# A decoder layer on one core: key weights split one product later, a store on another queue, sums in another ring, a shorter block of passes ahead of the first scores

## The chip, the cores and the metric

One Trainium2 chip, one of its cores. The metric is the device time of one execution in microseconds (us), the median of several runs. TensorE is the matrix engine (PE in the rows, its weight loads PEld), VectorE is DVE, ScalarE is ACT, GpSimd is POOL. SyncE (SP) issues nearly all transfers; its rows carry "SPq". A pass below is one matmul with 128 x 128 stationary and 512 moving columns.

## What is computed

One layer of a hybrid decoder, in float32, for one sequence of 1024 tokens and 1024 channels. Cut to what matters here:

```python
h = rms_norm(x, norm_mix_pre)
proj = h @ w_in                     # q_d | k_d | v_d | u_pool | q_mem | gate logits
a = diff_attention(q_d, k_d, v_d, lam)          # 8 heads, two softmax maps each
y_attn = rms_norm(a, subln_g) * (1 - lam_init) @ w_attn_branch
y_pool = multiscale_pool(u_p, ...) @ w_pool_branch
y_mem  = memory_cross_attention(q_m, ...) @ w_mem_branch
gates  = sigmoid(gate_logits)                   # three gates of 1024 channels
mix = gates[0] * y_attn + gates[1] * y_pool + gates[2] * y_mem
x = x + rms_norm(mix @ w_out, norm_mix_post)
x = x + rms_norm(conv_ffn(rms_norm(x, norm_ffn_pre)), norm_ffn_post)
```

The change lies between the gates of the pool and memory branches and the first head of the attention. Nothing of what is computed changes.

## The kernel before

Every float32 operand is split into two parts, hi and lo, that TensorE multiplies: `split` (lines 83 to 92) writes hi with ScalarE (line 86, or 89 with a scale) and lo with VectorE (line 87, or 90), and `mm3` (lines 94 to 97) makes three passes: hi by hi, hi by lo, lo by hi. The projection products of this part use Strassen-like schemes with seven products in place of eight. Pages of split weights go through two rings of two buffers each in the pool `wst` (tags "wh" and "wl", used in turn), raw weights through a ring "raw" of two there and one more buffer in the pool `grp`.

The order of instructions on each engine and of transfers on each queue is not the program's order alone. A planner takes the program's order as priority and lets an instruction go ahead when its own estimates say that inputs and buffers are ready; `tc.issue_after(ins)` holds an instruction behind another on the same engine. What is planned is then executed strictly in that order on each engine and each queue, with semaphores.

The stages around the change, in order of time:

1. **Gates of two branches** (lines 609 to 629, up to about 418 us). For four pairs of channel blocks and two branches, `seven` makes the gate logits into `g` (ring "g" of three buffers of 1 MB in the pool `gp_`), ScalarE takes the sigmoid (line 623), VectorE multiplies by the branch `y` (ring "y" of two buffers of 1 MB, line 624), and the second branch is added to the first (line 628). The sum `mix` is stored to `mixp_d` by SyncE's queue (line 629).
2. **Values** (lines 637 to 738, about 418 to 506 us). Four loads of 1 MB bring the value weights `vw` (line 644) into buffers of the rings "g" and "y". `value_product` (lines 655 to 664) splits four pages and makes 48 passes into four PSUM banks. The products go in the order B11, B21, T2, T1, T3, B22, T4; between them PSUM is copied or added into `vtmp` (ring "g") and back into `vw`. `value_combination` (line 681) makes sums of weight blocks on VectorE. `key_weights(h)` (lines 666 to 676) loads the weights of head h's keys (line 670), splits them into two pages of the same rings "wh" and "wl", and stores these to `wk_d` (line 676). It is called for heads 2 to 7: 2 after B11, 3 after B21, 4 after T2, 5 after T1, 6 after T3, 7 after B22.
3. **Keys and queries** (lines 740 to 772, about 506 to 627 us). `channels` calls `seven` for two channel blocks at a time; `split_heads` splits the result into `hl` (ring "y") and stores it (line 758). The first group and the last, gate channels C_G, keep their four weight sums `ss` in a buffer of the ring "y"; the others in the pool `gq`. `weight_sums` (lines 194 to 197) makes them.
4. **Start of the attention** (lines 1009 to 1070, from about 627 us). The gate of channel block 2 is a generator `gate(2)`, here `first`: 48 passes in four steps of 12, the second and fourth ending with a copy and a store (lines 867 and 868). Two of its steps stand ahead of the first scores (lines 1015 and 1024), and `first_scores` is held behind the last of their passes by `issue_after`. The other steps are fillers of head 0: `weave` deals fillers out among the stages of a head. Scores are line 898, their bias and minimum VectorE's line 901, the exponential line 906, the turned weights line 936, values line 953.

The bias of a head is made by ScalarE from a ramp that GpSimd writes (lines 784 to 791). The keys of head 0 are loaded by line 826, its queries by line 815, its values by line 804.

Of the kernel before, what the change touches and what calls it, by code (L numbers as in the profile page):

```python
# [8 lines left out]
F32 = mybir.dt.float32  # L9
# [6 lines left out]
P = 128  # L16
# [3 lines left out]
H4 = KT // 2  # L20
# [18 lines left out]
def kernel(  # L39
# [7 lines left out]
    nc = tc.nc  # L47
# [12 lines left out]
    out = out[0]  # L60
# [245 lines left out]
    mixp_d = dram.tile([KT, P, S], F32, name="mixp_d")  # L306
# [31 lines left out]
    def chunk(w, c0, n=P):  # L338
        return w[:, c0:c0 + n].rearrange("(k p) c -> p k c", p=P)
# [10 lines left out]
    with tc.tile_pool(name="kvm", reuse_waits="tile", bufs=1, side="right") as kvp:  # L350
# [59 lines left out]
        with tc.tile_pool(name="xa", reuse_waits="tile", bufs=2, side="right") as xa:  # L410
# [81 lines left out]
            for j in range(MH):  # L492
# [9 lines left out]
                fillers = [lambda i=i: pool_in(j, i) for i in range(2)]  # L502
# [106 lines left out]
    with tc.tile_pool(name="gp", reuse_waits="tile", bufs=2, side="right") as gp_:  # L609
        for dt in range(0, KT, 2):  # L610
            mix = None
            for b in (1, 0):
                raws = []
                for e in range(2):
                    w = (grp if e else wst).tile([P, KT, P], F32, tag="raw", name="rawg", bufs=2 - e)
                    nc.sync.dma_start(out=w, in_=chunk(w_in, C_G + (2 - b) * D + (dt + e) * P))
                    raws.append(w)
                y = gp_.tile([P, 2, S], F32, tag="y", name="y")
                nc.sync.dma_start(out=y, in_=branch_d[b][dt:dt + 2].rearrange("e p s -> p e s"))
                g = gp_.tile([P, 2, S], F32, tag="g", name="g", bufs=3)  # L620
                s12, s43 = [gq.tile([P, 2, H4, P], F32, tag="t", name="s") for _ in range(2)]
                seven(raws, (s12[:, 0], s12[:, 1], s43[:, 0], s43[:, 1]), hop, g)
                sigmoid = nc.scalar.activation(out=g, in_=g, func=AF.Sigmoid)
                nc.vector.tensor_tensor(out=g, in0=g, in1=y, op=ALU.mult)
                if b == 1:
                    mix = g
                else:
                    nc.vector.tensor_tensor(out=mix, in0=mix, in1=g, op=ALU.add)
            nc.sync.dma_start(out=mixp_d[dt:dt + 2].rearrange("e p s -> p e s"), in_=mix)

# [18 lines left out]
        def vblock(a, b):  # L651

            return [vw[a][k // 2][:, k % 2, b] for k in range(4)]

        def value_product(name, ws, acc, fresh):
            for k in range(4):
                page = wst.tile([P, 2, H], F32R, tag=("wh", "wl")[pages[0] % 2], name="vpage")
                pages[0] += 1
                split(page[:, 0], page[:, 1], ws[k])
                bh, bl = hop(name, k)  # L660
                for t in TS:
                    ts = slice(t * P, (t + 1) * P)
                    mm3(acc[t], bh[:, ts], bl[:, ts], page[:, 0], page[:, 1], fresh and k == 0, k == 3,
                        onto=not fresh)

        def key_weights(h):

            raw = wst.tile([P, KT, P], F32, tag="raw", name="rawk", bufs=2)
            with tc.issue_after(loads["v"].ins):
                nc.sync.dma_start(out=raw, in_=chunk(w_in, C_K + h * P))  # L670
            for e in range(2):
                page = wst.tile([P, 2, H4, P], F32R, tag=("wh", "wl")[pages[0] % 2], name="kpage")
                pages[0] += 1
                ks = slice(e * H4, (e + 1) * H4)
                split(page[:, 0], page[:, 1], raw[:, ks])
                nc.sync.dma_start(out=wk_d[h, :, :, ks], in_=page.bitcast(F32))
# [22 lines left out]

        A11, A21, A12, A22 = (0, 0), (0, 1), (1, 0), (1, 1)  # L700
        value_product("B11", vblock(*A11), va, True)
        key_weights(2)
        for t in TS:
            nc.scalar.activation(out=vtmp[:, t], in_=va[t], func=AF.Copy)
        value_product("B21", vblock(*A12), vb, True)
        key_weights(3)
        for t in TS:
            nc.vector.tensor_tensor(out=vtmp[:, t], in0=vb[t], in1=vtmp[:, t], op=ALU.add)
        value_combination(A21, A21, A22, ALU.add)
        value_combination(A11, A21, A11, ALU.subtract)  # L710
        value_product("T2", vblock(*A11), va, False)
        key_weights(4)
        for t in TS:
            value_out(t, 0, vtmp[:, t])
        value_product("T1", vblock(*A21), vb, True)
        key_weights(5)
        for t in TS:
            nc.scalar.activation(out=vtmp[:, t], in_=va[t], func=AF.Copy)
# [41 lines left out]
        ss = gp_.tile([P, 4, H4, P], F32, tag="y", name="ss")  # L760
# [1 line left out]
        for h in range(0, NH, 2):  # L762
            split_heads(channels(h * P), q_d[h:h + 2], -0.125)

        ss = gp_.tile([P, 4, H4, P], F32, tag="y", name="ss")
        g01 = [gq.tile([P, S], F32, tag="t", name="g01") for _ in range(2)]
        late = []
        channels(C_G, ss=[ss[:, j] for j in range(4)], g=g01, late=late)
# [237 lines left out]
    def steps(gen, n):  # L1006
        return [lambda: next(gen, None)] * n
# [5 lines left out]
    first = gate(2)  # L1013
# [7 lines left out]
    with tc.issue_after(last["load"].ins):  # L1021
        for dt in range(2):
            nc.sync.dma_start(out=gate_d[dt], in_=g01[dt])
    next(first)
    GATES = ((2,), (), (), (), (), (), (), (3,))
    blocks = [(h, b) for h in range(NH) for b in range(4)]
    for h in range(NH):
        stages = []
        for b in range(4):
            n = 4 * h + b  # L1030
            if n == 0:
                def first_scores():
                    with tc.issue_after(last["gate"].ins):
                        scores(0, 0, 0)
                stages.append(first_scores)
            else:
                stages.append(lambda h=h, b=b: scores(h, b, 0))
            if b == 1 and h + 1 < NH:
                stages.append(lambda h=h: head_bias(h + 1))
            if n >= 1:  # L1040
                def weights(n=n):
                    combine(*blocks[n - 1], 1)
                    turn_weights(*blocks[n - 1])
                stages.append(weights)
            stages.append(lambda h=h, b=b: scores(h, b, 1))
            stages.append(lambda h=h, b=b: combine(h, b, 0))
            if n >= 2:
                stages.append(lambda n=n: head_norm(*blocks[n - 2]))
            if n >= 1:
                stages.append(lambda n=n: weigh_values(*blocks[n - 1]))  # L1050
            if h == HG and b == 0:
                stages.append(lambda: turn_sums(0))
            if h == HG and b == 1:
                stages.append(lambda: load_norms(0))
            if h == HG and b == 3:
                def norms():
                    with tc.issue_after(last["combine"].ins):
                        head_norms(0)
                stages.append(norms)
            if b in (1, 3) and h + 1 < NH:  # L1060
                stages.append(lambda h=h, b=b: queries(h + 1, b // 2))
        fillers = []
        if h + 1 < NH:
            if h:
                fillers += steps(head_keys(h + 1), 4)
            for n, step in enumerate(steps(values(h + 1), 2)):
                fillers.insert(2 * n + 1, step)
        for dt in GATES[h]:
            fillers += steps(first if dt == 2 else gate(dt), 2 if dt == 2 else 4)
        weave(stages, fillers)  # L1070
    combine(*blocks[-1], 1)
    turn_weights(*blocks[-1])
# [47 lines left out]
    for dt in range(KT):  # L1120
        wh, wl, _ = wsplit(chunk(w_attn_branch, dt * P), [P, KT, P])
        for i in range(2):
            hs = slice(i * H, (i + 1) * H)
            gm2 = gq.tile([P, 2, H], F32, tag="t", name="gm2")
            g, mp = gm2[:, 0, :], gm2[:, 1, :]
# [66 lines left out]
    with tc.tile_pool(name="wo", reuse_waits="tile", bufs=1, side="right") as wo:  # L1192
# [3 lines left out]
        for t in range(KT):  # L1196
# [19 lines left out]
            y = yp.tile([P, D], F32, tag="y", name="y", bufs=3)  # L1216
# [284 lines left out]
```

## Time and profile before

| | |
|---|---|
| median of 3 runs | 1764.55 us (1763.64 to 1766.16) |
| profiled execution, time | 1765.92 us |
| its span in the trace | 1763.9 us |
| mean granted TensorE clock | 0.994 |
| TensorE matmul busy | 1718.4 us, 97% |
| VectorE busy | 1274.2 us, 72% |
| ScalarE busy | 884.4 us, 50% |
| GpSimd busy | 45.6 us, 3% |
| DMA share of SyncE's queue | 51.1% |

The busy times are of one profiled execution; the span is what the trace covers, and the execution's time lies 2 us above it. A wait is put down to the instruction or transfer that came last. In the rows a start is in us from the beginning of the span, a length in us, and a line of `split` or `mm3` is that of the helper, so the tile names tell the stage.

### The profile page before, as it was taken

To read this page: it belongs to the slowest core of one execution; us is meant where nothing else is said; L and a number is where in the kernel's file an instruction comes from. 1 tells how busy PE (TensorE), PEld (TensorE's weight loads), DVE (VectorE), ACT (ScalarE), POOL (GpSimd) and SP (SyncE) were. 2 spreads that over 40 slices of the span, in tenths; PEclk is the share of its full clock that TensorE was granted. 3 is DMA by queue.
4 is the path that set the end of the run, shared out by engine and by line. 5 is a ranking of instruction groups with operands and counts; after the bars stand their busy time and mean duration, and the time that the engine had idled before them with its cause. 6 is when DMAs were issued, how large, how long until landed. Compare 5 with 4: busy or idle time off the path is not lost.

```text
span 1763.9 us, 22641 instructions
## 1 busy us (share of the span) xinstructions
PE 1718.4 (97%) x8138; PEld 1424.6 (81%) x8138; DVE 1274.2 (72%) x2227; ACT 884.4 (50%) x1551; POOL 45.6 (3%) x103
## 2 busy tenths in 40 slices
PE   6999999997999999999999999999999999999997
PEld 5888888886888778888888888888888888788886
DVE  7766875665575567888865557858888888878476
ACT  6434454433444366777743333545555555543452
POOL 0000000000000011111110000000000000000000
PEclk9999999999999999999999999999999999999999
DMA  7784544454675576665556472374334323583343
GB/s 243 251 304 145 181 152 132 153 165 132 215 224 188 176 210 179 190 166 159 149 188 222 159 235 72 119 229 135 113 103 126 118 74 108 186 297 103 112 138 138
DMA packets 232933, 294.95 MB, mean 167 GB/s; under 512 B 15873, under 2 KB 161526, under 8 KB 230134
## 3 DMA queue, kind: packets, MB, share of 16 engines
q1 hardware_dynamic: 229302, 286.13, 51.1%
q0 software_dynamic: 3520, 7.38, 1.2%
q8 instruction: 64, 1.05, 0.2%
q14 instruction: 47, 0.39, 0.1%
HBM read 201.62 MB, written 85.56 MB: 163 GB/s over the span
## 4 chain that ended last, share of the span: by engine, by line
PE 75%; issue 13%; DVE 4%; DMA 4%; POOL 2%; ACT 2%; SPq 0%; POOLq 0%; DVEq 0%; ACTq 0%
PE pa L95 8%; PE pa L96 8%; PE pa L97 8%; PE pb L95 5%; PE pb L97 5%; PE pb L96 5%; PE pe L97 2%; PE pe L95 2%; PE pe L96 2%; PE pya L96 2%; PE pya L95 2%; PE pya L97 2%; PE pd L95 2%; PE pd L97 2%; PE pd L96 2%
## 5 line engine op out<-in xcount | busy, mean ns | idle before, releaser
L86 ACT ACTIVATE wpage<-s 128x512 fp32r<-128x512 f32 x136 | 85.2, 627 | 106.8 <-DVE s L194 42.8
L87 DVE TENSOR_TENSOR wpage<-s,wpage 128x512 fp32r<-128x512 f32 x136 | 92.7, 688 | 44.8 <-ACT wpage L86 44.8
L1279 DVE SCALAR_TENSOR_TENSOR cvt<-gv,cols,cvt 128x1023 f32<-128x1023 f32 x88 | 112.5, 1278 | 15.6 <-ACT cvt L1275 15.6
L901 DVE CUSTOM_DVE_ANT_0 z<-pss,hbias 128x256 f32<-128x256 f32 (+7 forms) x128 | 94.9, 752 | 27.9 <-PE pss L898 26.7
L906 ACT ACTIVATE z<-z,mx 128x256 f32<-128x256 f32 (+7 forms) x128 | 98.9, 774 | 21.3 <-DVE mx L901 21.1
L95 PE MATMUL pa<-T,wpage 128*128 128x512 f32 x264 | 102.8, 389 | 1.2 <-DVE gv L252 1.2
L96 PE MATMUL pa<-T,wpage 128*128 128x512 f32 x264 | 102.7, 389 | 0.0
L97 PE MATMUL pa<-T,wpage 128*128 128x512 f32 x264 | 102.7, 389 | 0.0
L898 PE MATMUL pss<-ks,q 128*128 128x512 f32 (+5 forms) x384 | 88.7, 352 | 1.2 <-DVE mx L901 1.2
L86 ACT ACTIVATE page<-blk 128x1024 fp32r<-128x1024 f32 (+1 forms) x42 | 41.4, 988 | 85.7 <-PE pe L96 50.6
L87 DVE TENSOR_TENSOR page<-blk,page 128x1024 fp32r<-128x1024 f32 (+1 forms) x42 | 47.5, 1131 | 38.6 <-ACT page L86 38.6
L898 PEld LDWEIGHTS pss<-ks,q 128*128 128x128 f32 x384 | 62.4, 189 | 12.3 <-DVE mx L901 7.6
L86 ACT ACTIVATE wh<-raw 128x1024 fp32r<-128x1024 f32 (+1 forms) x46 | 41.8, 910 | 60.5 <-PE pb L96 13.7
L95 PE MATMUL pd<-page 128*128 128x512 f32 x176 | 68.6, 390 | 1.7 <-ACT row L1389 1.7
L96 PE MATMUL pd<-page 128*128 128x512 f32 x176 | 68.5, 389 | 0.0
L97 PE MATMUL pd<-page 128*128 128x512 f32 x176 | 68.5, 389 | 0.0
L95 PE MATMUL pa<-hT,wpage 128*128 128x512 f32 x168 | 65.7, 391 | 0.1
L97 PE MATMUL pa<-hT,wpage 128*128 128x512 f32 x168 | 65.4, 389 | 0.0
L96 PE MATMUL pa<-hT,wpage 128*128 128x512 f32 x168 | 65.4, 389 | 0.0
L953 PEld LDWEIGHTS poa<-aT,v 128*128 128x128 f32 x480 | 60.5, 190 | 4.8 <-ACT srow L973 2.5
L953 PE MATMUL poa<-aT,v 128*128 128x256 f32 (+1 forms) x480 | 63.2, 281 | 0.8 <-ACT srow L973 0.5
L87 DVE TENSOR_TENSOR wl<-raw,wh 128x1024 fp32r<-128x1024 f32 (+1 forms) x46 | 47.6, 1034 | 18.5 <-ACT wh L86 18.4
(415 smaller groups left out, 5050.7 us busy)
## 6 DMA issues: line engine op xcount, KB each, us to landing
q<-q_d SPq DMA_DIRECT2D x64, 256.0 KB, 5.3
wd<-in_w_down_dram SPq DMA_DIRECT2D x22, 512.0 KB, 6.2
tw_d<-wd SPq DMA_DIRECT2D x11, 1024.0 KB, 4.5
rawv<-in_w_up_dram SPq DMA_DIRECT2D x22, 512.0 KB, 5.6
rawu<-in_w_up_dram SPq DMA_DIRECT2D x22, 512.0 KB, 3.9
ff_d<-cvt SPq DMA_DIRECT2D x22, 512.0 KB, 4.2
blk<-ff_d SPq DMA_DIRECT2D x20, 512.0 KB, 7.0
br<-tw_d SPq DMA_DIRECT2D x20, 512.0 KB, 3.5
```

The lines of the kernel that those rows point to most:

```text
L86: copy = nc.scalar.activation(out=hi, in_=src, func=AF.Copy)
L87: nc.vector.tensor_tensor(out=lo, in0=src, in1=hi.bitcast(F32), op=ALU.subtract)
L95: nc.tensor.matmul(o, ah, bh, start=first, stop=False, skip_group_check=onto)
L96: nc.tensor.matmul(o, ah, bl, start=False, stop=False, skip_group_check=onto)
L97: return nc.tensor.matmul(o, al, bh, start=False, stop=last, skip_group_check=onto)
L898: nc.tensor.matmul(pss[:, i * H:i * H + m], q[:, j, c, ts], keys, start=(j == 0), stop=(j == 1))
L901: nc.vector.tensor_tensor_reduce(out=halves(z[:, 0:n]), in0=pss.rearrange("p (a m) -> p a m", a=2)[:, 0:parts, 0:m], in1=halves(biases[h][ ...
L906: nc.scalar.activation(out=z[:, 0:n], in_=z[:, 0:n], func=AF.Exp, scale=-1.0, bias=mx[:, c:c + 1], accum_out=sm if c else sums[:, h, t:t + 1])
L953: nc.tensor.matmul(po[:, qs], (vh, vl)[i][:, k, :], w[j][:, ws], start=(n == 0), stop=(n == len(terms) - 1))
L1279: nc.vector.scalar_tensor_tensor(out=cv[:, sh:], in0=u[:, 0:S - sh], scalar=w, in1=cv[:, sh:], op0=ALU.mult, op1=ALU.add)
```

## The change

Four edits. The store of `mix` goes from SyncE's queue to GpSimd's. In the values stage the calls of `key_weights` for heads 2, 3 and 4 each move behind the next product, so that two of them (4 and 5) follow T1. The weight sums of the last group of channels go from the ring "y" to the ring "g". The second step of `first` is no longer made ahead of the first scores: it becomes a filler of head 0, which has three steps of it in place of two.

```diff
@@ gates of two branches
-            nc.sync.dma_start(out=mixp_d[dt:dt + 2].rearrange("e p s -> p e s"), in_=mix)
+            nc.gpsimd.dma_start(out=mixp_d[dt:dt + 2].rearrange("e p s -> p e s"), in_=mix)
@@ values
         value_product("B11", vblock(*A11), va, True)
-        key_weights(2)
         for t in TS:
             nc.scalar.activation(out=vtmp[:, t], in_=va[t], func=AF.Copy)
         value_product("B21", vblock(*A12), vb, True)
-        key_weights(3)
+        key_weights(2)
         for t in TS:
             nc.vector.tensor_tensor(out=vtmp[:, t], in0=vb[t], in1=vtmp[:, t], op=ALU.add)
         value_combination(A21, A21, A22, ALU.add)
         value_combination(A11, A21, A11, ALU.subtract)
         value_product("T2", vblock(*A11), va, False)
-        key_weights(4)
+        key_weights(3)
         for t in TS:
             value_out(t, 0, vtmp[:, t])
         value_product("T1", vblock(*A21), vb, True)
+        key_weights(4)
         key_weights(5)
@@ last group of channels
-        ss = gp_.tile([P, 4, H4, P], F32, tag="y", name="ss")
+        ss = gp_.tile([P, 4, H4, P], F32, tag="g", name="ss", bufs=3)
         g01 = [gq.tile([P, S], F32, tag="t", name="g01") for _ in range(2)]
@@ start of the attention
     with tc.issue_after(last["load"].ins):
         for dt in range(2):
             nc.sync.dma_start(out=gate_d[dt], in_=g01[dt])
-    next(first)
@@ fillers of a head
         for dt in GATES[h]:
-            fillers += steps(first if dt == 2 else gate(dt), 2 if dt == 2 else 4)
+            fillers += steps(first if dt == 2 else gate(dt), 3 if dt == 2 else 4)
```

## Rows read from the trace of the kernel before

**Rows 1.** The page, part 1: busy us, share of the span, instructions of each engine.
```profile
PE 1718.4 (97%) x8138; PEld 1424.6 (81%) x8138; DVE 1274.2 (72%) x2227; ACT 884.4 (50%) x1551; POOL 45.6 (3%) x103
```

**Rows 2.** Waits over the whole span: us in total, times, longest.
```profile
PE ve L95 <- ACT vpage L86: 9.8, 1, 9.8
PE pb L95 <- ACT wpage L86: 3.1, 1, 3.1
...
ACT vpage L86 <- DMA wk_d<-kpage: 12.2, 9, 2.5
```

**Rows 3.** Busy us of each engine in four stretches, then granted clock, DMA share, GB/s.
```profile
428.00:444.00 16.00, 6.20 (x19) 4.46 (x18) 9.28 (x10) 4.88 (x9) 0.00 (x0) 0.68 0.87 272
444.00:500.00 56.00, 56.00 (x249) 46.34 (x248) 37.58 (x57) 30.06 (x52) 0.00 (x0) 1.00 0.73 224
598.00:616.00 18.00, 14.91 (x53) 11.33 (x52) 8.74 (x12) 6.84 (x10) 0.00 (x0) 0.81 0.70 204
640.00:662.00 22.00, 19.36 (x118) 15.70 (x116) 19.83 (x47) 18.20 (x41) 3.94 (x7) 1.00 0.72 188
```

**Rows 4.** TensorE in order of time, end of product B11 and start of B21.
```profile
426.12 0.39 PE L97 MATMUL vd<-vpage,hTl 128*128 128x512 f32 x1
...
428.84 0.39 PE L97 MATMUL vd<-vpage,hTl 128*128 128x512 f32 x1
439.03 1.22 PE L95 MATMUL ve<-vpage,hTh 128*128 128x512 f32 x2 [9.80 <-ACT vpage L86]
...
443.45 0.39 PE L96 MATMUL ve<-vpage,hTh 128*128 128x512 f32 x1
```

**Rows 5.** The chain that ended last, between 400 and 660 us: start, us, what.
```profile
426.02 0.37 SPq L629
...
426.95 10.34 DMA rawk<-in_w_in_dram
```

**Rows 6.** ScalarE in order of time, around B11's end.
```profile
410.23 0.63 ACT L86 ACTIVATE vpage<-vw 128x512 fp32r<-128x512 f32 x1 [1.60 <-PE pb L97]
...
431.69 2.07 ACT L704 ACTIVATE vtmp<-vd 128x512 f32<-128x512 f32 x4 [8.86 <-DMA mixp_d<-g]
437.31 1.15 ACT L86 ACTIVATE kpage<-rawk 128x512 fp32r<-128x512 f32 x2 [3.56 <-DMA rawk<-in_w_in_dram]
```

**Rows 7.** VectorE in order of time, the first sums of value weights.
```profile
428.68 2.48 DVE L681 TENSOR_TENSOR vw<-vw 128x1024 f32<-128x1024 f32 x2 [2.72 <-DMA vw<-in_w_in_dram]
435.52 2.48 DVE L681 TENSOR_TENSOR vw<-vw 128x1024 f32<-128x1024 f32 x2 [4.36 <-DMA vw<-in_w_in_dram]
```

**Rows 8.** DMA issues: tiles, queue, count, KB each, median us to landing.
```profile
mixp_d<-g SPq DMA_DIRECT2D x4, 1024.0 KB, 5.0
...
rawq<-in_w_in_dram SPq DMA_DIRECT2D x12, 512.0 KB, 4.0
...
ks<-k_d SPq DMA_DIRECT2D x8, 256.0 KB, 8.9
```

**Rows 9.** Line 868, GpSimd's stores of 256 KB: issue to landing.
```profile
DMA to landing us min/median/max: 2.3/5.2/8.2
```

**Rows 10.** TensorE in order of time, second product of the last group.
```profile
608.02 0.80 PE L95 MATMUL pb<-hT,wpage 128*128 128x512 f32 x1 [3.09 <-ACT wpage L86]
...
614.27 0.40 PE L97 MATMUL pa<-hT,wpage 128*128 128x512 f32 x1
```

**Rows 11.** VectorE in order of time, first weight sum of the last group.
```profile
606.62 0.69 DVE L194 TENSOR_TENSOR ss<-rawq 128x512 f32<-128x512 f32 x1 [1.36 <-DMA q_d<-hl]
```

**Rows 12.** SyncE's queue in order of time: last weights of that group, second keys.
```profile
593.24 0.38 SPq L745 DMA_DIRECT2D rawq<-in_w_in_dram  x1
...
618.64 1.08 SPq L826 DMA_DIRECT2D ks<-k_d  x2
```

**Rows 13.** TensorE in order of time, the first scores.
```profile
632.89 0.56 PE L898 MATMUL pss<-ks,q 128*128 128x128 f32 x4
```

**Rows 14.** ScalarE in order of time, the biases of two heads.
```profile
628.20 2.21 ACT L791 ACTIVATE hbias<-bias 128x1152 f32<-128x1152 f32 x2
```

## The prediction

> **What bounds the kernel now.** I read the busy shares first: TensorE is busy for 97% of the span [rows 1], so the end is set by its passes and by the places where it has none to make. The waits come next, to find these places. In the part that the change touches there are two long ones: 9.8 us at the first pass of product B21 of the values, and 3.1 us at the second product of the last group of channels [rows 2]. The windows show what each costs beyond the wait: from 428 to 444 us TensorE is busy for 6.20 of 16 us at a mean granted clock of 0.68, from 598 to 616 us for 14.91 of 18 at 0.81; between them, from 444 to 500 us, it never stops [rows 3]. Head 0 of the attention is the third place: 19.36 of 22 us, with VectorE at 19.83 [rows 3].
>
> *The first stall.* Twelve passes go from 426.12 to 428.84, so a pass at the full clock takes 0.227 us. The next starts at 439.03 after 9.80 us of waiting, and the ten from there to 443.45 take 4.42 us where 2.27 would do [rows 4]: the clock had gone to its lower level of 1.2 GHz in the pause. The stall is worth 9.80 + 2.15 = 11.95 us. The chain says why: SyncE's queue issues the store of `mix` at 426.02, and a load of key weights takes from 426.95 on, 10.34 us [rows 5]. ScalarE stands in its order: copies of `vtmp` at 431.69 after 8.86 us of waiting for the store's landing, then key pages at 437.31 after 3.56 us for their load, and only behind these the page that TensorE needs [rows 6]. The data of that page had been there much longer: VectorE reads the third block of value weights at 428.68, the fourth at 435.52 [rows 7].
>
> *The second stall.* At 606.62 VectorE can write the first weight sum, because a store out of the ring "y" has landed [rows 11]; the pass follows at 608.02. From there to 614.27 are 14 passes, 6.25 us for 3.18 [rows 10]: 3.09 + 3.07 = 6.16 us.
>
> **The change, part by part.** No pass is added or taken away; all of it is order and waiting.
>
> *Key weights one product later.* The pair of key pages, and the wait for their load, leave ScalarE's queue between B11 and B21. What is late next: the page of B21 needs the third block of weights (here at 428.68), a free buffer (the first of B11 is used up after a quarter of B11), and its turn on ScalarE. The turn is the choice to be made. The copies of `vtmp` come first in the program and wait for the store. But the planner lets pages go ahead: the first page of B11 was split at 410.23, almost 8 us before its first pass and ahead of copies of the product before [rows 6]. I take it that the first two pages of B21 go ahead of the copies. Then hi is ready at 428.68 + 0.63 = 429.3, a page's time on ScalarE [rows 6]. Lo takes VectorE 0.69 us, like any two-input instruction of 128x512 [rows 11], behind at most one sum of 1.24 [rows 7]: 430.0 to 430.6. B11 ends at 429.07; TensorE loses 0.7 to 1.3 us, I take 1.2. These two pages feed 24 passes, 5.4 us, to about 436.0. The third page needs the fourth block (435.52) and its turn behind the `vtmp` copies (2.07 us after the store has landed): hi at 436.2 to 437.2, lo at 436.9 to 438.5 behind a sum. TensorE loses 0.9 to 2.5 us, I take 1.6. Of 11.95 us some 2.8 remain: **a gain of 9.1 us**; 11.2 if the first pause alone is left, 6.0 if both are at their long ends and the clock falls once more (2.15).
>
> *Heads 4 and 5 together behind T1.* Eight pages in a row want the rings. ScalarE waits nine times, 12.2 us in all, for stores of key pages already [rows 2], and TensorE has no pause in that stretch [rows 3], so the cover is there. It gets thinner by two pages of 0.63 us on ScalarE and 0.69 on VectorE in one product of 48 x 0.227 = 10.9 us. The second page of T3 becomes late first. I take a **loss of 0.3 us**, between 0 and 1. The stores to `wk_d` and the loads of raw weights move along on SyncE's queue; what they store is needed in the attention only.
>
> *The store on GpSimd's queue.* SyncE's queue is no longer held for VectorE's last addition, but the load behind it there takes a buffer that this addition frees, so 0.4 us of issue time [rows 5] is what it gets. By the code GpSimd's next instruction after these stores is the bias ramp of the attention (line 784), so nobody stands behind the store's wait. What may differ is the landing: 5.0 us now [rows 8], for GpSimd's stores 2.3 to 8.2 at a quarter of the size [rows 9]. From 426.3 that is 431.3 to 434.5; it is in the bounds above, because only the `vtmp` copies wait for it. Where the three earlier stores are issued TensorE has no long wait [rows 2], and I cost them at nothing; their cover is a branch's 84 passes, 19 us.
>
> Of the Trainium skill two rules speak on this. The page DMA: Bandwidth & Descriptors (Queues, rings and completion order) says that a DMA engine takes turns between queues packet by packet; by it the store would no longer go ahead of the fourth block but share with it. With the landing of [rows 8] the third page would cost 0.9 us and the sum be 16.8; by the rule, at the late end, 2.5 us and 15.2. The page SBUF — State Buffer (Summary: rules for kernel authors) says that descriptors of GpSimd's transfers starve while VectorE runs in a two-port mode; that is the last rival below.
>
> *Weight sums in the ring "g".* Its three buffers hold the outputs of the query groups, of which two are in use at once, so one is free a group of 84 passes, 19 us, ahead. The sums can start when the weights are there: the load issued at 593.24 [rows 12] takes 4.0 us [rows 8], so at 597.3, ten us before 606.62. Four sums and a page are 4 x 0.69 + 0.63 + 0.69 = 4.1 us, done by 602 even with VectorE's other work, and the pass is due at 608.02 - 3.09 = 604.9 [rows 10]. The whole wait goes and the clock stays: **a gain of 6.1 us**, 5.0 if a page is just late. Next on the path are the loads for head 0, and they are covered (below).
>
> *Twelve passes instead of 24 ahead of the scores.* The scores start 2.72 us earlier, and the 12 passes must fit in head 0. TensorE is idle there for 2.64 us of 22, VectorE for 2.17 [rows 3]. If all fit into pauses the gain is 2.6 us; if they stand in front of scores for which VectorE waits, it is a loss of up to 1. I take **a gain of 1.2 us**, near the middle, since the stage's limit is VectorE, which starts earlier but has little slack.
>
> *Sum.* 9.1 - 0.3 + 6.1 + 1.2 = 16.1 us. The profiled execution took 1765.92 us, 2.0 more than its span, and would take 1749.8. It lies 1.4 us above the median of the runs, 1764.55, which gives 1748.4. Behind these places TensorE has few pauses, so what is saved stays saved.
>
> **The rivals.**
> A: *the copies stay in front.* ScalarE makes the four `vtmp` copies before the pages of B21. The store's landing at 431.3 to 434.5, plus 0.4 + 2.07 + 0.63, lets TensorE start at 434.4 to 437.6: a gain of 4.6 to 1.4 us in place of 9.1. For it: program order, and that they are in front now. Against it: the order of [rows 6]. At 2.8 us, the sum is 9.8: 1754.8 us. Chance 0.18.
> B: *head 0 isn't fed.* The scores come at 632.89 - 6.16 - 2.72 = 624.0 on the clock of [rows 13], without the first stall's shift, which is common to all. The second keys, issued at 618.64 and so at 612.5, land 8.9 us later, at 621.4 [rows 8, 12]; the bias of head 0, 628.20 - 6.16 + 1.16 = 623.2 [rows 14]. It is enough by 0.8 to 2.6 us, but the stores of the last queries don't move, and a queue 5 us longer costs 3 us: 1751.5. Chance 0.13.
> C: *the ring doesn't give.* If the buffer of the ring "g" that the planner picks is freed late, the 6.1 us stay: 1754.5. That would be the change not doing what it says. Chance 0.05.
> D: *the planner gives it back.* New estimates reorder later stages; head 0 to head 7 and the down projection hold all other idle time. If 15 us are lost there: about 1763.5. No row shows it; the kernel is at 97% under the same planner [rows 1]. Chance 0.06.
> E, slower: *the store starves.* Place: the `vtmp` copies behind GpSimd's store. If it lands late, ScalarE blocks all pages behind. The other edits give 7.0 us, so the kernel is slower by over 0.2% (3.5 us) once TensorE starts after 439.03 + 7.0 + 3.5 = 449.5, that is at a landing after 446, 20 us from issue; at 22 us, 1770. The longest landing of GpSimd's queue is 8.2 us [rows 9], and VectorE is idle for 2.72 us just as the store is issued [rows 7]. Chance 0.04. The rule of the SBUF page is this mechanism; by the trace it has a free gap of VectorE to pass through.
>
> **How the numbers follow.** My forecast has 0.54 and its own range is 1744.5 to 1755.5, from gains of 20 (11.2 + 6.2 + 2.6) and 9 (6.0 - 1.0 + 5.0 - 1.0). With most of A, B and C the range that should hold 8 times in 10 is 1744.5 to 1757.5. What a measurement can tell from no change is about 0.2%. Faster by more than that are the forecast, A, B and C but for their tails: 0.87. Same: D and tails, 0.08. Slower: E and a bad end of D, 0.05.
>
> **What would show it.** In the changed kernel's trace the wait at the first pass of B21 is under 2 us and the granted clock stays 1.0 from 420 to 440 us; on ScalarE pages of B21 stand before line 704. If line 704 is first, A holds. The wait of `pb` on `wpage` at the last group is gone, and the sums start near 597 us less the first gain. The first scores come 2.7 us after the first gate pass; a wait of line 898 or 901 for `ks`, `q` or `hbias` there means B. Wrong altogether would be a store that takes over 10 us, or new waits of TensorE behind 660 us.

## The result and the profile after

The changed kernel takes 1771.58 us (median of 9 runs, 1767.49 to 1774.63) against 1766.15 us for the kernel before on the same chip: a ratio of 1.0031, with a 95% interval of 1.0018 to 1.0043. It is slower by some 5.5 us, where 1748.4 us had been forecast. The profiled execution took 1771.58 us, its span is 1769.8 us.

The first view is where each stage ends. The table gives the start of certain passes on TensorE, in us of each profiled span; each is the first or last start that the view of one tile lists.

| mark | before | after | difference |
|---|---|---|---|
| first pass of B11 of the values (`vd`) | 418.2 | 428.3 | +10.1 |
| last pass of the values (`vd`) | 506.3 | 515.1 | +8.8 |
| first gate pass ahead of the scores (`pg`) | 627.5 | 630.5 | +3.0 |
| last scores (`pss`) | 884.5 | 889.2 | +4.7 |
| span | 1763.9 | 1769.8 | +5.9 |

So ten microseconds are lost ahead of the values, nearly all in the gates stage. The values get back 1.3 of the 9 that were forecast, the ring gives its 6, and the attention loses 1.7. The busy shares say nothing of it (they answer to [rows 1]):

```profile
PE 1722.2 (97%) x8138; PEld 1426.2 (81%) x8138; DVE 1274.3 (72%) x2227; ACT 884.6 (50%) x1551; POOL 48.6 (3%) x107
```

The waits of the changed kernel, us in total, times, longest, answer to [rows 2]. The one long wait for `vpage` has shrunk from 9.8 to 3.9 us, that of `pb` is gone, and there is a new one, four times, for `wpage`:

```profile
PE pa L95 <- ACT wpage L86: 7.3, 4, 3.3
PE ve L95 <- ACT vpage L86: 3.9, 1, 3.9
```

The windows of the changed kernel (busy us of PE, PEld, DVE, ACT, POOL; granted clock, DMA share, GB/s) answer to [rows 3], with one more ahead, the gates stage:

```profile
300.00:417.00 117.00, 110.21 (x478) 90.20 (x477) 71.38 (x90) 46.70 (x69) 2.34 (x3) 0.99 0.39 125
428.00:444.00 16.00, 15.87 (x69) 12.47 (x69) 9.72 (x8) 5.56 (x7) 0.72 (x1) 1.00 0.57 185
444.00:500.00 56.00, 50.32 (x204) 39.59 (x203) 34.15 (x51) 27.65 (x50) 0.00 (x0) 0.94 0.73 224
598.00:616.00 18.00, 18.00 (x80) 14.75 (x79) 11.05 (x16) 8.25 (x13) 0.00 (x0) 1.00 0.39 132
640.00:662.00 22.00, 19.66 (x113) 16.31 (x112) 19.32 (x47) 17.30 (x39) 3.27 (x6) 0.97 0.79 239
```

In the kernel before the gates window had no gap at all:

```profile
300.00:417.00 117.00, 117.00 (x518) 96.92 (x517) 76.06 (x96) 49.66 (x74) 0.00 (x0) 1.00 0.39 131
```

**The gates stage.** VectorE of the changed kernel in order of time, as the first group after a store begins. Line 221 adds the bank `pa` into `g`; the last product of the group, T4, adds its passes on to the same bank, so it can't start before line 221 has read it. Line 194 makes the first weight sum of the next group:

```profile
316.62 0.69 DVE L87 TENSOR_TENSOR wpage<-rawg,wpage 128x512 fp32r<-128x512 f32 x1
322.66 0.69 DVE L194 TENSOR_TENSOR s<-rawg 128x512 f32<-128x512 f32 x1 [5.35 <-DMA rawg<-in_w_in_dram]
323.27 0.68 DVE L221 TENSOR_TENSOR g<-pa,g 128x512 f32<-128x512 f32 x1
```

The same place in the kernel before:

```profile
317.75 0.69 DVE L221 TENSOR_TENSOR g<-pa,g 128x512 f32<-128x512 f32 x1 [1.36 <-PE pa L97]
319.45 0.69 DVE L194 TENSOR_TENSOR s<-rawg 128x512 f32<-128x512 f32 x1 [1.01 <-DMA rawg<-in_w_in_dram]
```

The two have changed places. The weight sum waits 5.35 us for its load, and the addition, whose data has long been there, stands behind it. TensorE of the changed kernel stops at T4, which needs the bank:

```profile
320.96 0.39 PE L97 MATMUL pc<-hTh,wpage 128*128 128x512 f32 x1
324.10 0.47 PE L95 MATMUL pa<-hT,wpage 128*128 128x512 f32 x1 [2.75 <-ACT wpage L86]
```

The profile puts this wait down to the page, but the page's last part was written by VectorE at 316.62. What came at 323.95 is the end of line 221. This happens after each of the three earlier stores: the sum waits 5.35, 5.92 and 3.33 us for its load, and TensorE 2.75, 3.32 and 0.72 us for the addition behind it, each time 2.6 us less; 6.8 us in all. So with the sum in front some 2.6 us of its wait cost nothing, and the rest is TensorE's. The kernel before shows the harmless side: in two of the groups that no store precedes the sum stands in front there already, waits 1.54 and 1.63 us, and TensorE has no gap:

```profile
336.97 0.69 DVE L194 TENSOR_TENSOR s<-rawg 128x512 f32<-128x512 f32 x1 [1.54 <-DMA rawg<-in_w_in_dram]
337.58 0.69 DVE L221 TENSOR_TENSOR g<-pa,g 128x512 f32<-128x512 f32 x1
```

Of the 10.1 us at the first pass of B11 another 0.9 was there before the first store (line 628 first starts at 310.8 against 309.9). Most of the rest is the clock after the second wait; the window of it:

```profile
345.00:385.00 40.00, 36.68 (x155) 29.88 (x155) 21.90 (x28) 14.96 (x22) 0.74 (x1) 0.96 0.40 132
```

It has 155 passes where the kernel before has 178. At 0.227 us a pass these are 5.2 us, of which 3.32 are the wait.

**The values.** ScalarE of the changed kernel (answers to [rows 6]): two pages of B21 stand ahead of line 703, the copies of `vtmp`, as forecast. But the copies wait until 446.78, and the third page stands behind them:

```profile
438.75 1.15 ACT L86 ACTIVATE vpage<-vw 128x512 fp32r<-128x512 f32 x2 [5.84 <-DMA vw<-in_w_in_dram]
446.78 2.07 ACT L703 ACTIVATE vtmp<-vd 128x512 f32<-128x512 f32 x4 [6.88 <-DMA mixp_d<-g]
448.71 1.17 ACT L86 ACTIVATE vpage<-vw 128x512 fp32r<-128x512 f32 x2
```

The chain of waits (answers to [rows 5]; start, us, what) has the store there:

```profile
436.58 10.09 DMA mixp_d<-g
```

TensorE (answers to [rows 4]) loses 3.94 us for that page:

```profile
449.41 0.79 PE L95 MATMUL ve<-vpage,hTh 128*128 128x512 f32 x1 [3.94 <-ACT vpage L86]
```

It then loses part of its clock: from 444 to 500 us it is busy for 50.32 us at a mean of 0.94. The median store takes 7.6 us in place of 5.0, the weight loads of the gates, which come beside them, 6.6 in place of 5.5 (DMA issues, answers to [rows 8]):

```profile
rawg<-in_w_in_dram SPq DMA_DIRECT2D x16, 512.0 KB, 6.6
mixp_d<-g POOLq DMA_DIRECT2D x4, 1024.0 KB, 7.6
```

**The ring.** The second product of the last group starts without a wait (answers to [rows 10]):

```profile
614.22 0.39 PE L95 MATMUL pb<-hT,wpage 128*128 128x512 f32 x1
```

**The first scores.** In the kernel before the first four score passes, two for each softmax map, stand together [rows 13]. In the changed kernel moved gate passes stand between the two maps (TensorE in order of time, line 898 alone):

```profile
633.26 0.33 PE L898 MATMUL pss<-ks,q 128*128 128x128 f32 x2
636.01 0.62 PE L898 MATMUL pss<-ks,q 128*128 128x128 f32 x4
```

VectorE in the same stretch waits twice, 5.03 us for the first map and 2.34 for the second:

```profile
633.74 0.29 DVE L901 CUSTOM_DVE_ANT_0 z<-pss,hbias 128x128 f32<-128x128 f32 x1 [5.03 <-PE pss L898]
636.38 0.29 DVE L901 CUSTOM_DVE_ANT_0 z<-pss,hbias 128x128 f32<-128x128 f32 x1 [2.34 <-PE pss L898]
```

From the first gate pass to the second of these it is 5.5 us; to the first four of the kernel before it was 5.4. So the second map starts no earlier than it did.

### The profile page after: what moved, and what is told of

It is laid out like the page before. It is cut to its first block, busy times and chain, and to the rows that moved or that the text cites. A ratio compares the mean times of both kernels' runs of the same rounds, so it can differ in the third digit from the quotient of the medians.

```text
span 1769.8 us, 22658 instructions
## 1 busy us (share of the span) xinstructions
PE 1722.2 (97%) x8138; PEld 1426.2 (81%) x8138; DVE 1274.3 (72%) x2227; ACT 884.6 (50%) x1551; POOL 48.6 (3%) x107
## 4 chain that ended last, share of the span: by engine, by line
PE 80%; DVE 9%; DMA 5%; ACT 3%; issue 2%; SPq 0%; DVEq 0%; ACTq 0%; POOLq 0%
PE pa L95 7%; PE pa L97 7%; PE pa L96 7%; PE pb L95 5%; PE pb L97 5%; PE pb L96 5%; PE pss L898 2%; PE poa L953 2%; PE pe L96 2%; PE pe L95 2%; PE pe L97 2%; PE pya L95 2%; PE pya L97 2%; PE pya L96 2%; PE pd L95 2%
```

## The experiments

Theory: the edits of the key weights and of the ring do what was forecast. The store on GpSimd's queue costs more than both bring, in two ways: the three earlier stores upset the order on VectorE, and the last one lands late. Rivals: the loads behind the stores are late as such, whatever the order; any second queue does the same; or the edits cost through each other.

All runs in one table. Each ratio is against the kernel before, run alongside, whose median lay between 1765.31 and 1768.24 us. The two marks are of the profiled execution: the first gate pass `pg`, and the time from it to the last scores.

| kernel | median us | ratio (95%) | first `pg` | to last scores |
|---|---|---|---|---|
| before | 1766.15 | 1 | 627.5 | 257.0 |
| after | 1771.58 | 1.0031 (1.0018 to 1.0043) | 630.5 | 258.7 |
| e1_all_but_store | 1755.19 | 0.9932 (0.992 to 0.9945) | 612.7 | 258.5 |
| e2_store_only | 1778.88 | 1.0076 (1.0062 to 1.009) | 635.6 | 258.1 |
| e3_ring_only | 1762.36 | 0.9979 (0.997 to 0.9988) | 621.4 | 257.0 |
| e4_passes_only | 1767.41 | 1.0007 (0.9996 to 1.0017) | 627.0 | 258.3 |
| e5_keys_and_ring | 1753.58 | 0.9925 (0.9911 to 0.994) | 611.9 | 257.3 |
| e6_store_sums_held | 1768.41 | 1.0016 (1.0004 to 1.0027) | 629.9 | 257.1 |
| e7_last_store_only | 1759.20 | 0.9963 (0.9949 to 0.9977) | 617.9 | 259.3 |
| e8_store_act_queue | 1765.80 | 1.0002 (0.9991 to 1.0012) | 626.8 | 257.0 |
| e9_after_sums_held | 1758.16 | 0.9958 (0.9944 to 0.9971) | 618.2 | 259.2 |
| e10_act_queue_in_after | 1757.55 | 0.9952 (0.9939 to 0.9966) | 616.5 | 258.0 |
| e11_36_passes | 1755.56 | 0.9937 (0.9923 to 0.995) | 611.7 | 259.7 |
| e12_keys_only | 1757.69 | 0.9948 (0.9931 to 0.9966) | 618.1 | 257.2 |

Four medians lie a little outside the range of the theory behind them: all but the store 2.2 us above it, the store alone 0.9 above, the two runs with the last store alone (e7) and with the sums held in the changed kernel (e9) 0.8 below. The ring alone lies between its theory and its rival.

**Four parts apart: all but the store.** Against the changed kernel:

```diff
-            nc.gpsimd.dma_start(out=mixp_d[dt:dt + 2].rearrange("e p s -> p e s"), in_=mix)
+            nc.sync.dma_start(out=mixp_d[dt:dt + 2].rearrange("e p s -> p e s"), in_=mix)
```

> The three edits without the store: mix stays on SyncE's queue. Theory (the store on GpSimd's queue is what loses): the gates stage is as before, without waits of TensorE between 300 and 417 us; the third page of B21 waits for the store's landing some 5 us after its issue and not 10, so TensorE loses 1 to 3 us between B11 and B21's end where the kernel before loses 12; the last group loses nothing. Gains 9 + 6 and nothing or 1 to 2 us lost by the moved passes: 1750 to 1753 us against 1766 of the kernel before. Rival (another edit loses, or the moved order as such): 1763 to 1772, and waits stay in the values or appear in the attention.

One word back on SyncE's queue brings 16.4 us. TensorE is busy for 116.66 us of the gates window.

**The store alone.** Against the kernel before, the same word the other way:

```diff
-            nc.sync.dma_start(out=mixp_d[dt:dt + 2].rearrange("e p s -> p e s"), in_=mix)
+            nc.gpsimd.dma_start(out=mixp_d[dt:dt + 2].rearrange("e p s -> p e s"), in_=mix)
```

> The store of mix alone goes to GpSimd's queue. Theory (store): three stalls in the gates stage as in the changed kernel, 9 us, and the copies of vtmp wait for a landing of 10 us, which the load of key weights hides but for 1 to 2 us: 1774 to 1778 us. The landing of the weight loads behind the store is 7 to 8 us where it was 5.3 to 5.8. Rival (the store is harmless alone, the gates stalls come from the other edits through the planner): 1766, no waits in the gates stage.

It costs 0.76%, some 13 us. Waits of this run and its gates window:

```profile
PE ve L95 <- ACT vpage L86: 10.4, 1, 10.4
PE pa L95 <- ACT wpage L86: 6.7, 3, 3.1
```

```profile
300.00:417.00 117.00, 110.33 (x478) 90.32 (x477) 71.28 (x90) 47.81 (x71) 2.34 (x3) 0.99 0.40 130
```

The three waits are there without the other edits, so they are the store's own.

**The ring alone, and the passes alone.** Against the kernel before:

```diff
-        ss = gp_.tile([P, 4, H4, P], F32, tag="y", name="ss")
+        ss = gp_.tile([P, 4, H4, P], F32, tag="g", name="ss", bufs=3)
```

> The weight sums of the last group alone move to the ring g. Theory: the wait of 3.1 us and the slow passes behind it go, 6 us, and nothing behind takes them back: 1760 us. Rival (taken back at the start of the attention, where the loads of head 0 don't come earlier): first scores wait for keys, 1764 to 1766.

```diff
-    next(first)
...
-            fillers += steps(first if dt == 2 else gate(dt), 2 if dt == 2 else 4)
+            fillers += steps(first if dt == 2 else gate(dt), 3 if dt == 2 else 4)
```

> The 12 passes alone go behind the first scores. Theory (the planner puts them back, between the scores of the first and the second softmax map, because it takes the second keys to land later): VectorE starts no earlier counted from the first gate pass (5.9 us), and nothing is gained: 1765 to 1768 us, the upper end if the reordered head 0 costs 1.6 us as in the changed kernel. Rival (the gain of 1.2 us that was forecast, hidden by the other edits): 1764 to 1765 and VectorE 2.7 us earlier.

The ring brings 6.1 us up to the first gate pass (627.5 to 621.4), but by the medians 3.7 us (2.1 to 5.3). The passes bring nothing that can be measured; by the marks they cost 1.3 us between the gate and the last scores. In the six kernels with 12 passes ahead this stretch takes 258.0 to 259.3 us; in the seven with 24 it takes 257.0 to 257.3, but for the store alone, 258.1. The loss shows from 22 to 40 us behind the first gate pass. First the passes alone, then the kernel before:

```profile
649.00:667.00 18.00, 14.53 (x87) 11.82 (x85) 15.38 (x41) 14.54 (x35) 2.65 (x5) 0.91 0.52 159
649.50:667.50 18.00, 15.22 (x97) 11.68 (x95) 16.84 (x46) 15.04 (x37) 2.83 (x6) 1.00 0.57 162
```

TensorE is idle for 0.7 us more, and the clock falls. The fall isn't bound to this edit: the store alone has it too (0.91 in the same stretch), and the changed kernel with ScalarE's queue, with 12 passes, hasn't (1.00). Why the moved order leaves more pauses there stays open.

**The key weights alone.** Against the kernel before, the hunk of the change in the values stage:

```diff
-        key_weights(2)
...
-        key_weights(3)
+        key_weights(2)
...
-        key_weights(4)
+        key_weights(3)
...
+        key_weights(4)
         key_weights(5)
```

> The key weights one product later, alone. It splits the gain of the pair (0.9925 of before, 12.2 us of 1765.7) into its terms. The run with the ring alone gave 0.9979, 3.7 us, where the prediction had 6.1 for the ring and 8.8 for the key weights. Theory 1 (the ring is worth 3.7 us): this takes 0.9952 of before, 1757.2 us. Theory 2 (the ring is worth 6 us and the run alone lost 2 us elsewhere): 0.9965 to 0.997, 1759.5 to 1760.5 us. In both, TensorE's wait at the first pass of B21 is under 2 us and the 3.1 us wait of `pb` in the last group stays.

It takes 0.9948 of before, 9.2 us (6.0 to 12.2), and 9.4 us by the first gate pass. The median, 1757.69 us, is close to the 1757.2 of theory 1. Two of its windows, the first the stretch of B21:

```profile
428.00:444.00 16.00, 14.68 (x60) 10.57 (x59) 14.42 (x20) 9.63 (x17) 0.00 (x0) 1.00 0.87 274
598.00:616.00 18.00, 17.23 (x63) 13.61 (x64) 8.54 (x14) 5.71 (x9) 2.81 (x3) 0.81 0.74 186
```

With the store on SyncE's queue TensorE loses 1.3 us where it had lost 9.8, and the clock stays; the loss of the last group (clock 0.81) is still there, as only the ring removes it.

**Key weights and ring.** Against the run with all but the store, the 24 passes ahead of the scores again:

```diff
+    next(first)
...
-            fillers += steps(first if dt == 2 else gate(dt), 3 if dt == 2 else 4)
+            fillers += steps(first if dt == 2 else gate(dt), 2 if dt == 2 else 4)
```

> The key weights one product later and the ring alone; the store stays on SyncE's queue, 24 passes stay ahead of the first scores. Theory: the 12 moved passes are worth nothing or cost a little (the order of scores and passes eats the 2.7 us), so this is at least as fast as the run with all but the store (1755.19): 1753.9 us, between 1753 and 1755.5, and the stretch from the first gate pass to the last score of the attention takes 257.0 us as in the kernel before, not 258.5. Rival, by the prediction: the moved passes are worth 1.2 us, and without them it is 1756.4 us.

1753.58 us, the fastest of all: 12 us better than before, 18 than the changed kernel. The gate-to-scores stretch is 257.3 us, as the theory has it; by the medians the 1.6 us between this run and e1 lie inside both intervals.

**The order on VectorE.** The store alone, with the weight sums held behind the addition:

```diff
+    freed = {}
...
-        a11, a12, a21, a22 = weight_sums(raws, ss)
+        with (tc.issue_after(freed["pa"].ins) if "pa" in freed else ExitStack()):
+            a11, a12, a21, a22 = weight_sums(raws, ss)
...
-        nc.vector.tensor_tensor(out=c22, in0=pa, in1=c21, op=ALU.add)
+        freed["pa"] = nc.vector.tensor_tensor(out=c22, in0=pa, in1=c21, op=ALU.add)
```

> The store alone on GpSimd's queue, as in the run that took 1778.88 us; in addition the weight sums of a group of seven products (line 194) are held on VectorE behind the addition that empties the bank `pa` of the group before (line 221). Theory (the order on VectorE): the three waits of TensorE for the pages behind the bank `pa` in the gates, 6.7 us and some 2 us of lower clock, come from a weight sum that waits for its late load ahead of that addition; with the order held they go, 1770 us, and TensorE is busy for at least 116 of 117 us from 300 to 417 us. Rival (the transfers): the loads behind the store land at 7.7 us in place of 5.3 and the pages made from them are late whatever the order; then TensorE waits for the same pages or for those of the next product, 1777 to 1779 us.

10.5 us come back. VectorE of this run (the lines are shifted: 223 is the addition, 195 the sum):

```profile
317.56 0.69 DVE L223 TENSOR_TENSOR g<-pa,g 128x512 f32<-128x512 f32 x1 [1.36 <-PE pa L97]
321.75 0.69 DVE L195 TENSOR_TENSOR s<-rawg 128x512 f32<-128x512 f32 x1 [3.49 <-DMA rawg<-in_w_in_dram]
```

```profile
300.00:417.00 117.00, 116.83 (x515) 96.10 (x514) 75.48 (x96) 49.51 (x74) 2.33 (x3) 1.00 0.41 131
```

The load is as late as in the changed kernel (321.75 against 322.66, which was 0.9 us behind already), and the sum still waits for it; only the addition doesn't stand behind the sum now. So late loads cost next to nothing by themselves here, as the order by itself cost nothing in the kernel before: it takes both. The same hold in the changed kernel:

> The changed kernel (1771.58 us) with the weight sums of a group of seven products held on VectorE behind the addition that empties the bank `pa`. Theory (the loss of the three earlier stores is the order on VectorE): TensorE's waits for `wpage` between 300 and 417 us go, 9 to 12 us come back, and what is left against the run in which only the last store goes by GpSimd's queue (1759.2) is 0 to 3 us: 1759 to 1762.5 us. The wait of 3 to 4 us for the third page of product B21 stays, since the last store lands as late as before. Rival (late loads as such, hidden in the run with the store alone by other waits): 1765 us or more.

1758.16 us, 13.4 less than the changed kernel and as fast as the run with the last store alone, below. The rival falls in both. The hold by itself brings nothing. In the gates the kernel before has no gap to give back, and from the last pass of the values to the first gate pass, where `seven` is used too, it is 121.2 us before and 121.3 with the hold (629.9 - 508.6).

**The last store alone.** The changed kernel with three stores back on SyncE's queue:

```diff
-            nc.gpsimd.dma_start(out=mixp_d[dt:dt + 2].rearrange("e p s -> p e s"), in_=mix)
+            (nc.gpsimd if dt == 6 else nc.sync).dma_start(out=mixp_d[dt:dt + 2].rearrange("e p s -> p e s"), in_=mix)
```

> All four edits, but of the four stores only the last (channel blocks 6 and 7) goes by GpSimd's queue. Theory: the three earlier stores cost the gates stage 9 us and the last one 5 to 7 us in the values stage, so this stands between the run with all but the store (1755.19) and the changed kernel (1771.58): 1760 to 1762 us, no wait of TensorE for `wpage` between 300 and 417 us, and the last store lands some 10 us after issue with a wait of 3 to 4 us for the third page of product B21. Rival: the last store alone is late only because the loads around it were already late; then it lands in 5 to 8 us and the time is 1755 to 1757 us.

It has no wait in the gates (117.00 of 117 us), a wait of 3.3 us for the third page, 5.2 us at the first gate pass against the run with all but the store. The store lands 9.3 us after issue, and the copies start at 436.44. The window of B21, and the DMA queues (packets, MB, share of 16 engines) in the microsecond from 433 to 434, in this run:

```profile
428.00:444.00 16.00, 12.32 (x45) 8.92 (x44) 10.78 (x12) 5.37 (x11) 0.00 (x0) 0.91 0.72 237
```

```profile
q0 software_dynamic: 90, 0.37, 89.4%
q1 hardware_dynamic: 95, 0.05, 16.0%
```

q0 holds GpSimd's store, q1 SyncE's loads. From 427 to 432, five microseconds after the issue at 427.00, q1 has all of the 462 packets. Then the two take turns: 90 packets against 95, but the store's are of 4 KB and the load's of 0.5 KB, so the load gets an eighth of the bytes. The page DMA: Bandwidth & Descriptors (Queues, rings and completion order) of the Trainium skill says that an engine takes turns between queues packet by packet, and in this stretch the trace agrees. In the gates of the changed kernel it doesn't show so: from 318 to 319 us the store has 105 packets and the load none.

**Another second queue.** The store alone, on ScalarE's queue:

```diff
-            nc.sync.dma_start(out=mixp_d[dt:dt + 2].rearrange("e p s -> p e s"), in_=mix)
+            nc.scalar.dma_start(out=mixp_d[dt:dt + 2].rearrange("e p s -> p e s"), in_=mix)
```

> The kernel before with the store of `mix` on ScalarE's queue instead of SyncE's, all four of them. Theory A (any other queue): store and load go at the same time, the weight loads of the gates land in 7 to 8 us instead of 5.3, and TensorE waits for `wpage` as with GpSimd's queue: 1774 us or more. Theory B (GpSimd's own issue, 0.55 us after VectorE's end and 0.72 to 0.88 us long, and how its transfers are served): on ScalarE's queue the loads land in 5.5 us and the gates have no such waits: 1764 to 1769 us, with ScalarE's own wait for VectorE's addition as the only cost.

Time as before (ratio 1.0002), no gap in the gates: theory B by the time, and for the most part by the loads: from 300 to 418 us the median weight load lands in 4.9 us, against 5.3 before and 7.8 in the changed kernel. Right behind a store theory A has a part of it. VectorE of this run:

```profile
318.94 0.69 DVE L221 TENSOR_TENSOR g<-pa,g 128x512 f32<-128x512 f32 x1 [1.89 <-PE pa L97]
321.48 0.69 DVE L194 TENSOR_TENSOR s<-rawg 128x512 f32<-128x512 f32 x1 [0.26 <-DMA rawg<-in_w_in_dram]
```

The first sum after a store starts 2 us later than before (319.45), but here the planner has left the addition in front. For the last store ScalarE shows what the queue itself costs:

```profile
434.57 2.07 ACT L704 ACTIVATE vtmp<-vd 128x512 f32<-128x512 f32 x4 [11.66 <-DMA mixp_d<-g]
```

Issued at 426.08, it is waited for until 434.57, 8.5 us. On SyncE's queue that was 426.02 to 431.69, 5.7 us [rows 5, 6]; on GpSimd's 427.00 to 436.44, 9.4 us. In the microsecond from 431 to 432 the store (q10) and the loads share evenly, now with packets of one size:

```profile
q10 hardware_dynamic: 54, 0.22, 53.9%
q1 hardware_dynamic: 50, 0.20, 49.9%
```

The changed kernel with that queue:

> The changed kernel with ScalarE's queue in place of GpSimd's for all four stores. Theory: with ScalarE's queue the gates lose nothing, and the last store lands some 8.5 us after VectorE's last addition (5.7 on SyncE's queue, 10 on GpSimd's), so the copies of `vtmp` start near 434.5 us, the third page of B21 is 1 to 2 us late, and the time is 1755.2 (all but the store) plus 1 to 2: 1756 to 1757.5 us. Rival (any queue but SyncE's upsets the planner's order once the other three edits are in): waits for `wpage` between 300 and 417 us and 1765 us or more.

1757.55 us, the wait for the third page 1.7 us: the theory. Both other queues give up the store's place ahead of the loads; GpSimd's adds a later start.

**More passes ahead.** Against key weights and ring:

```diff
     next(first)
+    next(first)
...
-            fillers += steps(first if dt == 2 else gate(dt), 2 if dt == 2 else 4)
+            fillers += steps(first if dt == 2 else gate(dt), 1 if dt == 2 else 4)
```

> The key weights and the ring as in the run that took 1753.58 us, and the number of gate passes ahead of the first scores changed the other way: 36 in place of 24, one step of 12 left as a filler of head 0. Theory: 24 is near the best, since with 12 the passes stood between the scores of the two maps and cost 1.2 us, and with 36 the scores, for which VectorE waits, come 2.7 us later: 1754 to 1756 us, and 258 to 260 us from the first gate pass to the last score in place of 257. Rival (the fewer fillers head 0 has, the better): 1751.5 to 1753 us and 255.5 to 256.5.

259.7 us from gate to last scores, against 257.3 with 24 passes and 258.0 to 259.3 with 12. The marks put 24 below both neighbours, though the store alone, with 24, has 258.1; the medians (1755.56 and 1753.58) can't tell them apart.

## Why the prediction was wrong

The first gate pass can be followed from kernel to kernel: 627.5 before; 618.1 with the key weights; 611.9 with the ring too; 612.7 with the passes; 617.9 with the last store on GpSimd's queue; 630.5 with all four stores. The terms are 9.4, 6.2, -0.8, -5.2 and -12.6 us. Each is from one profile of a kernel. In the kernels that lose less than half a microsecond in the gates the first pass of B11 lies anywhere from 417.5 to 419.2 us, so a term as small as the -0.8 of the passes says nothing.

- **The key weights: right.** 9.1 - 0.3 = 8.8 us were forecast, 9.4 came. The choice that pages go ahead of the copies held (rival A falls), and so did the cover of heads 4 and 5.
- **The three earlier stores: the step that failed.** They were costed at nothing, with a branch's 84 passes as cover. Those passes cover a page, not the order on VectorE. The planner put a weight sum ahead of the addition that reads `pa`, and the sum waited 3.3 to 5.9 us for a load behind the store; what passed 2.6 us TensorE lost. That the planner's estimates of the transfers made the order is not shown, as no trace holds them; that the order changed with the store's queue, and that holding it gives the loss back, is. The three stores cost 12 us (0.9963 to 1.0031) and turned the sign. The row that asked for a look stood in the waits of the kernel before:

```profile
DVE s L194 <- DMA rawg<-in_w_in_dram: 7.6, 5, 2.1
```

VectorE was waiting for these very loads five times already, 2.1 us at most. TensorE was kept out of it in two ways: behind the stores the addition went first, and elsewhere the waits stayed below 2.6 us. In the changed kernel the same row reads 19.9 us, six times, 5.9 at most.
- **The last store's landing: mis-sized.** 431.3 to 434.5 was taken, from 5.0 us for this store on SyncE's queue to 8.2 for GpSimd's stores of 256 KB. It took 10.09 us, just past the 10 that the prediction had named as a sign of being wrong altogether, and the third page cost TensorE 3.94 us and some clock where 1.6 was allowed: 5.2 us at the first gate pass in the run with that store alone.
- **The ring: right by its place, open by its sum.** 6.1 us were forecast and 6.1 came by the first gate pass; rival C falls. The medians show 3.7 alone, and 3.0 on top of the key weights (12.2 less 9.2, each with some 3 us of uncertainty). Behind the last pass of `pout` lies a stretch that no edit touches, and in the profiled executions of all these kernels it takes 641.4 to 648.9 us (643.7 with the ring alone, 641.9 before); where the other 2.4 us go in a typical execution, one profile each doesn't tell.
- **The 12 passes: wrong sign.** +1.2 us was taken, -1.3 us shows in the stretch from gate to scores of the run with the passes alone. The step took the first score to be what VectorE waits for. In fact the passes went between the two maps, so VectorE had one map's first block early and then waited 2.34 us for the second. That explains why nothing was gained; the loss itself shows 22 to 40 us behind the first gate pass, in pauses and clock, and its cause is open. Rival B, late keys or bias, did not come: no score waited for `ks`, `q` or `hbias`.
- **The rivals.** Slower came by another way than E: the store didn't starve for 20 us (5.3 to 10.1 us to landing). It came by D's mechanism, a new order by the planner, which had 0.06 and was looked for in later stages, not beside the moved store itself.

## What to carry to other kernels

Where a planner fixes the order, moving a transfer to another queue can change the order on engines that never touch it: look, on each in-order engine, for an instruction that waits for a transfer and stands beside one that TensorE waits for, see which goes first, and read from the rows how much wait is free. A cover in passes says that a page has time; it says nothing of an instruction that may come to stand behind a wait. In these runs the store ahead of the loads on their own queue landed in 5.0 us in the median; on either second queue the last store started behind them and then shared with them.

## What the runs showed of the hardware

GpSimd's queue began late: with the last store alone on it the first packets of that store moved after 432, five microseconds from the issue at 427.00; on ScalarE's queue the first came between 428 and 429 for an issue at 426.08, while loads were still moving too. What holds GpSimd's store back isn't shown. The issue itself took GpSimd 0.72 to 0.88 us, where SyncE's row has 0.37. In the stretches from 433 to 434 and from 431 to 432 the two queues moved near the same number of packets (90 and 95, 54 and 50), so packets of 4 KB took seven eighths of the bytes from packets of 0.5 KB; in the gates, from 318 to 319 us, the store moved alone.
